# Moving small edge-row copies from GpSimd to ScalarE in a fused Mamba-2 and pooling decoder step

## The chip, the cores and the metric

The kernel runs on one core of a Trainium2 chip. The core's engines work side by side and meet through semaphores: TensorE multiplies matrices (PE for its multiplications, PEld for the loads of its stationary operand), VectorE (DVE), ScalarE (ACT) and GpSimd (POOL) work elementwise on tiles of up to 128 partitions, and SyncE (SP) issues the transfers between memory and the tiles. Each engine works through its own list of instructions in order.

The metric is the device time of one execution in microseconds. The kernel before took 1685.69 us, the median of three runs (1685.56 to 1687.11). The profile shows one more execution, of 1685.18 us.

## What is computed

One step of a decoder of two layers, on 1024 new prompt tokens and on 8 x 8 sample tokens that continue eight older sequences: 1088 token columns. Layer 0 is a Mamba-2 (SSD) mixer, layer 1 a causal pooling mixer; each is normalised, modulated, gated and added to its input. Beside the outputs y, the step returns the new states. Three parts matter here: the causal convolution of width 4 with the last three rows of its input as new state, the windowed means with the last 15 rows of their input as new state, and the input projections that produce both inputs.

```python
# SSD branch; conv_prev is zero for the prompt and state_conv for the samples
zxbcdt = h @ w_in
xbc = zxbcdt[..., D_INNER:D_INNER + CONV_DIM]
xp = jnp.concatenate([conv_prev, xbc], axis=1)
conv = conv_b + sum(xp[:, k:k + L] * conv_w[k] for k in range(4))
new_conv = xp[:, -3:]
xbc_act = jax.nn.silu(conv)          # then the SSD scan, gate, norm, w_out
...
# pooling branch; pool_prev is zero for the prompt and state_pool for the samples
uz = h @ w_in
u, z = uz[..., :2048], uz[..., 2048:]
up = jnp.concatenate([pool_prev, u], axis=1)
cs = jnp.cumsum(up, axis=1)          # with a zero row ahead
for g, w in enumerate((2, 4, 8, 16)):
    win_sum = cs[:, 16:16 + L, sl] - cs[:, 16 - w:16 - w + L, sl]
    pooled[g] = win_sum / cnt - u[..., sl]
mixed = (pooled @ w_group) * ch_scale * jax.nn.silu(z)
return mixed @ w_out, up[:, -15:]
```

The sizes: model width 1024, inner width 2048, convolution width (x, B and C together) 4096 = 32 tiles of 128 channels, pooling width 2048 = 16 tiles of 128 channels. Everything is float32.

## The kernel before

**Layout and precision.** Channels lie on the 128 partitions, tokens on the free axis: a tile is 128 channels by 1088 tokens, the 1024 prompt tokens first. Each float32 factor of a multiplication is held as a rounded high half and a low half of the rest, and each product is three multiplications, high x high, high x low and low x high: L168 to L170 in plain products, which go over the tokens in the chunks `CH` of 364, 364 and 360, and L922 to L924 in fast ones. ACT makes the high half by a copy with rounding, another engine subtracts it from the source to get the low half.

**Fast products.** Pairs of output tiles of the input projections are made by a Strassen-like scheme (`fast_pair`) that forms both tiles from seven half-size products. Each product (`product`) is 2 chunks x 4 blocks x 3 = 24 multiplications of 272 tokens. Its weights are sums and differences of blocks of the two tiles' weights, named `sw` and `wr`, which POOL works out in `w_sums` (L887, L888, L892, L894). Each of the seven then goes through `split_half`: the high half `hi` on ACT (L160), the low half `lo` by a subtraction (L162), on POOL for every split whose number modulo 7 is 3 or 5, on DVE for the other five. The tiles `w` for the split halves have two tags with two buffers each, so that three splits are made ahead of the product that uses them; a split can begin once the product that used its buffer is over. The partial results are read from PE's accumulators by ACT (L948) and added by DVE (L933).

**The stages**, by the time in the profiled execution:
- up to about 270 us: normalisation, the first plain products, then eight fast pairs (`front_pairs`): six of the gate z, and two of the convolution's inputs, whose four tiles make group 0.
- about 270 to 870 us: the scan of group g over its chunks of tokens (`scan_group`) is woven with the projection of group g + 1 (`proj_group`). A group is four convolution tiles; each takes three chunks of plain products, which ACT brings from the accumulators into the tile `raw` (L376 and, for the sample tokens of the last chunk, L378), and then the convolution (`conv_tile`). The scan of the next group begins with transpositions on PE (L509) of the convolution's outputs `xbc`. The exponentials of the scan are ACT's (L516, L534).
- about 870 to 1040 us: the output projection of layer 0.
- about 1040 to 1075 us: two plain pairs of layer 1; 1075 to 1360 us: its other fourteen pairs as fast products (`fast_pairs`), each 7 x 24 = 168 multiplications. A pair is one tile `u` of the pooled input and one of the gate, `pz`. The gate takes a tanh on ACT (L803) and a step on DVE (L804). The pairs come in order of their windows: pairs 0 to 3 window 4, then 8, 16 and 2, four pairs each.
- about 1360 us to the end: the product with `w_group`, the output projection and the last normalisation.

**The convolution tile.** `raw` is 128 x 1115: three columns of state (zeros), 1024 prompt columns, then eight sample sequences of three state columns and eight token columns, 11 each. `proj_begin` clears the three columns on POOL (L354) and copies the sample states from `scv` (L355). `scv` holds the states of a group, and is loaded by SP in `proj_open` (L347) into one of two buffers. `conv_tile` makes the first product on ACT (L332, from `raw` into a second tile `acc`, which has the name raw too), the other three on DVE (L334), copies the new state, 3 prompt columns (L335) and 8 x 3 sample columns (L336), from `raw` into `ncv`, then lets ACT overwrite `raw` by the tanh (L337), and DVE forms the output (L338, L340). The copies must therefore be done before L337. SP stores `ncv` after a group's fourth tile (L363).

**The pooled tile.** `u` is 128 x 1223: 15 columns of zeros, 1024 prompt columns, then 8 sequences of 15 state and 8 token columns. `u_begin` takes a buffer from the wide slots (seven, shared with the sums `ws`), has SP load `spl`, clears 15 columns on POOL (L761) and copies the 8 x 15 states (L762). The fast pair writes the tokens. `u_pool` copies the new state, 15 prompt columns (L777) and 8 x 15 sample columns (L778), into `npl`, which SP stores (L779), and then works on DVE: one to four doubling additions over the whole tile (L784, into `ws`), a correction of the first columns (L789), and the scaling and subtraction into `pl` (L791, L793). After these the buffers of `u` and `ws` are free for a later tile.

**Order.** The framework's scheduler turns the program into one list for each engine, by its own estimate of when things are ready; the program's order alone does not tell an engine's order. On the queues this matters for what stands behind what: SP's list holds the weight loads, the loads and the stores above; ACT's holds the splits' high halves, the tanh steps and the reads from the accumulators.

Of the kernel before, what the change touches and what calls it, by code (L numbers as in the profile page):

```python
# [83 lines left out]
class Build:  # L84
# [241 lines left out]
    def conv_tile(self, ti, raw, dst, ncv):  # L326

        nc, n = self.nc, 1112
        rv = raw[:, 1027:1115].rearrange("p (b w) -> p b w", w=11)
        w = [self.cwh[:, 4 * ti + k:4 * ti + k + 1] for k in range(4)]  # L330
        acc = self.raw_tile()
        nc.scalar.activation(acc[:, :n], raw[:, :n], AF.Identity, bias=self.cwh[:, 128 + ti:129 + ti], scale=w[0])  # L332
        for k in range(1, 4):
            nc.vector.scalar_tensor_tensor(out=acc[:, :n], in0=raw[:, k:k + n], scalar=w[k], in1=acc[:, :n], op0=ALU.mult, op1=ALU.add)  # L334
        nc.gpsimd.tensor_copy(ncv[:, 0:1, :], raw[:, 1024:1027].unsqueeze(1))  # L335
        nc.gpsimd.tensor_copy(ncv[:, 1:9, :], rv[:, :, 8:11])  # L336
        nc.scalar.activation(raw[:, :n], acc[:, :n], AF.Tanh)  # L337
        nc.vector.scalar_tensor_tensor(out=dst[:, :NP], in0=raw[:, :NP], scalar=1.0, in1=acc[:, :NP], op0=ALU.add, op1=ALU.mult)  # L338
        th, v = (t[:, 1027:1115].rearrange("p (b w) -> p b w", w=11)[:, :, 0:8] for t in (raw, acc))
        nc.vector.scalar_tensor_tensor(out=dst[:, NP:TOK].rearrange("p (b i) -> p b i", i=8), in0=th, scalar=1.0, in1=v, op0=ALU.add, op1=ALU.mult)  # L340
# [10 lines left out]
    def proj_begin(self, G, ii):  # L351
        nc = self.nc
        raw = self.raw_tile()
        nc.gpsimd.memset(raw[:, 0:3], 0.0)  # L354
        nc.gpsimd.tensor_copy(raw[:, 1027:1115].rearrange("p (b w) -> p b w", w=11)[:, :, 0:3], G["scv"][:, ii])  # L355
        return raw

    def proj_end(self, G, ii, raw):
# [396 lines left out]
    def u_begin(self, p):  # L755
        nc = self.nc
        raw = self.slots.get("u", wide=True)
        spl = self.gp2.tile([P, 8, 15], F32, tag="spl", bufs=2, name=self.name("spl"))
        nc.sync.dma_start(spl, self.io["spool"][p])
        rv = raw[:, 1039:1223].rearrange("p (b w) -> p b w", w=23)  # L760
        nc.gpsimd.memset(raw[:, 0:15], 0.0)  # L761
        nc.gpsimd.tensor_copy(rv[:, :, 0:15], spl)  # L762
        return raw, rv

    def u_chunk(self, U, ps, ch):
# [6 lines left out]
    def u_pool(self, p, U):  # L772

        nc, gi, (raw, rv) = self.nc, p // 4, U
        w = WINDOWS[gi]
        npl = self.gp2.tile([P, 9, 15], F32, tag="npl", bufs=2, name=self.name("npl"))
        nc.gpsimd.tensor_copy(npl[:, 0:1, :], raw[:, 1024:1039].unsqueeze(1))  # L777
        nc.gpsimd.tensor_copy(npl[:, 1:9, :], rv[:, :, 8:23])  # L778
        nc.sync.dma_start(self.io["npT"][p], npl)  # L779
        s, step, m = raw, 1, WIDE  # L780
        while step < w:
            d = self.slots.get("ws", wide=True)
            m -= step
            nc.vector.tensor_tensor(out=d[:, :m], in0=s[:, :m], in1=s[:, step:step + m], op=ALU.add)  # L784
            if step > 1:
                self.slots.free(s)
            s, step = d, 2 * step
        o = 16 - w
        nc.vector.tensor_tensor(out=s[:, o:o + w - 1], in0=s[:, o:o + w - 1], in1=self.kc[:, K_CNT + 15 * gi:K_CNT + 15 * gi + w - 1], op=ALU.mult)  # L789
        pl = self.slots.get("pl")  # L790
        nc.vector.scalar_tensor_tensor(out=pl[:, :NP], in0=s[:, o:o + NP], scalar=1.0 / w, in1=raw[:, 15:1039], op0=ALU.mult, op1=ALU.subtract)  # L791
        sv = s[:, 1039:1223].rearrange("p (b w) -> p b w", w=23)[:, :, o:o + 8]
        nc.vector.scalar_tensor_tensor(out=pl[:, NP:TOK].rearrange("p (b i) -> p b i", i=8), in0=sv, scalar=1.0 / w, in1=rv[:, :, 15:23],  # L793
                                       op0=ALU.mult, op1=ALU.subtract)
        self.slots.free(raw, s)
        nc.sync.dma_start(self.pld[p], pl)
        self.slots.free(pl)
# [764 lines left out]
```

## Time and profile before

| What | us |
|---|---|
| median of three runs (lowest, highest) | 1685.69 (1685.56, 1687.11) |
| the profiled execution | 1685.18 |
| its span in the profile | 1683.4 |
| busy PE / PEld | 1649.9 / 1556.7 |
| busy DVE / ACT / POOL | 1274.0 / 785.5 / 446.0 |

By stage, in the same execution (busy us):

| stretch, us | PE | DVE | ACT | POOL |
|---|---|---|---|---|
| 0 to 270 | 260.74 | 213.89 | 128.05 | 77.01 |
| 270 to 870 | 594.08 | 471.67 | 400.60 | 140.96 |
| 870 to 1040 | 169.37 | 111.57 | 56.17 | 18.04 |
| 1040 to 1075 | 32.09 | 32.29 | 23.08 | 12.73 |
| 1075 to 1360 | 282.57 | 262.54 | 92.02 | 173.37 |
| 1360 to 1683 | 311.02 | 182.07 | 85.54 | 23.86 |

Busy time counts an engine's instructions, not those that issue transfers or wait. The span runs from the first to the last recorded instruction; the execution's time has 1.78 us more around it. The granted clock of PE was 0.992 of full speed on the mean. A group of instructions is shown as line, engine, operation, output and input by the program's names, partitions x elements of each and the count, then the total and the mean of one in ns, then idle time of the engine just before and what ended it. In the view by time, the first number is the start and the second the duration, both in us; a bracket holds the idle time before it and what ended that. In the view of waits a row gives the waiting engine, tile and line, what it waited for, then the total in us, how often, and the longest.

### The profile page before, as it was taken

To read this page: it belongs to the slowest core of one execution; us is meant where nothing else is said; L and a number is where in the kernel's file an instruction comes from. 1 tells how busy PE (TensorE), PEld (TensorE's weight loads), DVE (VectorE), ACT (ScalarE), POOL (GpSimd) and SP (SyncE) were. 2 spreads that over 40 slices of the span, in tenths; PEclk is the share of its full clock that TensorE was granted. 3 is DMA by queue.
4 is the path that set the end of the run, shared out by engine and by line. 5 is a ranking of instruction groups with operands and counts; after the bars stand their busy time and mean duration, and the time that the engine had idled before them with its cause. 6 is when DMAs were issued, how large, how long until landed. Compare 5 with 4: busy or idle time off the path is not lost.

```text
span 1683.4 us, 30188 instructions
## 1 busy us (share of the span) xinstructions
PE 1649.9 (98%) x11771; PEld 1556.7 (92%) x11771; DVE 1274.0 (76%) x2182; ACT 785.5 (47%) x1539; POOL 446.0 (26%) x467
## 2 busy tenths in 40 slices
PE   8999999999999999999999999999999999999997
PEld 6899999889898888888889998999999999999997
DVE  6897688777778778788787647999999876555545
ACT  6544336767657676767442227533332343122123
POOL 0134440313122231222010022376666620000012
PEclk9999999999999999999999999999999999999998
DMA  8422225445354544445875132132333467411102
GB/s 336 164 89 104 78 80 207 146 145 182 108 171 121 167 127 141 141 123 182 285 247 192 43 116 79 67 125 97 111 110 110 138 250 305 155 52 51 38 26 106
DMA packets 111246, 232.03 MB, mean 138 GB/s; under 512 B 16864, under 2 KB 56960, under 8 KB 111104
## 3 DMA queue, kind: packets, MB, share of 16 engines
q1 hardware_dynamic: 111104, 230.10, 40.2%
q8 instruction: 93, 1.52, 0.4%
q14 instruction: 49, 0.40, 0.1%
HBM read 172.09 MB, written 57.98 MB: 137 GB/s over the span
## 4 chain that ended last, share of the span: by engine, by line
PE 34%; POOL 8%; issue 8%; DVE 5%; DMA 1%; ACT 1%; POOLq 0%; SPq 0%; ACTq 0%; DVEq 0%
PE mm L168 9%; PE mm L169 9%; PE mm L170 9%; POOL w L162 2%; PE st L924 1%; PE st L923 1%; PE st L922 1%; POOL sw L888 1%; POOL sw L887 1%; POOL npl L777 1%; POOL wr L892 1%; POOL npl L778 1%; DVE gl L684 1%; POOL sw L894 1%; PE y L550 0%
## 5 line engine op out<-in xcount | busy, mean ns | idle before, releaser
L168 PE MATMUL mm<-gh,wh 128*128 128x364 f32 (+3 forms) x768 | 254.8, 333 | 1.7 <-DVE x L703 1.3
L169 PE MATMUL mm<-gl,wh 128*128 128x364 f32 (+3 forms) x768 | 254.0, 331 | 2.2 <-DVE gl L684 2.2
L170 PE MATMUL mm<-gh,wl 128*128 128x364 f32 (+3 forms) x768 | 253.7, 331 | 0.0
L168 PE MATMUL mm<-hh,wh 128*128 128x364 f32 x720 | 248.4, 345 | 0.0
L169 PE MATMUL mm<-hl,wh 128*128 128x364 f32 x720 | 239.0, 332 | 0.0
L170 PE MATMUL mm<-hh,wl 128*128 128x364 f32 x720 | 237.6, 330 | 0.0
L703 DVE SCALAR_TENSOR_TENSOR x<-mm,gat,x 128x364 f32<-128x364 f32 (+3 forms) x192 | 108.9, 571 | 148.3 <-PE mm L170 147.9
L924 PE MATMUL st<-hh,w 128*128 128x272 f32 x704 | 203.2, 289 | 0.8 <-DVE w L162 0.8
L923 PE MATMUL st<-hl,w 128*128 128x272 f32 x704 | 203.1, 288 | 0.0
L922 PE MATMUL st<-hh,w 128*128 128x272 f32 x704 | 202.9, 288 | 0.0
L125 ACT ACTIVATE wh<-wr 128x1024 fp32r<-128x1024 f32 x73 | 77.2, 1057 | 224.6 <-PE mm L169 209.1
L924 PE MATMUL st<-t,w 128*128 128x272 f32 x528 | 152.4, 289 | 3.8 <-POOL w L162 2.9
L923 PE MATMUL st<-t,w 128*128 128x272 f32 x528 | 152.2, 288 | 0.7 <-DVE t L1190 0.7
L922 PE MATMUL st<-t,w 128*128 128x272 f32 x528 | 151.7, 287 | 0.0
L168 PEld LDWEIGHTS mm<-gh,wh 128*128 128x128 f32 x768 | 144.8, 189 | 5.4 <-DVE x L703 2.0
L169 PEld LDWEIGHTS mm<-gl,wh 128*128 128x128 f32 x768 | 145.4, 189 | 3.8 <-DVE gl L684 2.8
L170 PEld LDWEIGHTS mm<-gh,wl 128*128 128x128 f32 x768 | 145.5, 189 | 0.3 <-issue 0.2
L563 POOL TENSOR_TENSOR hd<-h,cd 128x256 f32<-128x256 f32 x56 | 67.1, 1198 | 282.4 <-DVE h L564 139.4
L334 DVE SCALAR_TENSOR_TENSOR raw<-raw,cwh,raw 128x1112 f32<-128x1112 f32 x96 | 134.3, 1399 | 9.8 <-ACT raw L332 9.1
L168 PEld LDWEIGHTS mm<-hh,wh 128*128 128x128 f32 x720 | 135.4, 188 | 5.5 <-ACT raw L376 1.6
L169 PEld LDWEIGHTS mm<-hl,wh 128*128 128x128 f32 x720 | 135.5, 188 | 4.6 <-issue 3.0
L170 PEld LDWEIGHTS mm<-hh,wl 128*128 128x128 f32 x720 | 135.3, 188 | 3.0 <-issue 2.9
(267 smaller groups left out, 4060.7 us busy)
## 6 DMA issues: line engine op xcount, KB each, us to landing
wr<-win SPq DMA_DIRECT2D x48, 512.0 KB, 4.8
acb<-acd SPq DMA_DIRECT2D x64, 256.0 KB, 3.9
wr<-pin SPq DMA_DIRECT2D x32, 512.0 KB, 3.6
x<-xT SPq DMA_DIRECT2D x16, 544.0 KB, 7.3
zsd<-z SPq DMA_DIRECT2D x16, 544.0 KB, 2.7
z<-zsd SPq DMA_DIRECT2D x16, 544.0 KB, 5.8
gyd<-xbc SPq DMA_DIRECT2D x16, 544.0 KB, 4.9
gr<-gyd SPq DMA_DIRECT2D x16, 544.0 KB, 4.9
```

The costliest lines, as they stand in the source:

```text
L125: self.nc.scalar.activation(hi[:, :nk, :], raw[:, :nk, :], AF.Copy)
L162: eng.tensor_tensor(out=lo, in0=src, in1=hi.bitcast(F32), op=ALU.subtract)
L168: nc.tensor.matmul(ps[:, :n], hi[:, k, :], ah[:, a:a + n], start=first, stop=False)
L169: nc.tensor.matmul(ps[:, :n], hi[:, k, :], al[:, a:a + n], start=False, stop=False)
L170: nc.tensor.matmul(ps[:, :n], lo[:, k, :], ah[:, a:a + n], start=False, stop=last)
L334: nc.vector.scalar_tensor_tensor(out=acc[:, :n], in0=raw[:, k:k + n], scalar=w[k], in1=acc[:, :n], op0=ALU.mult, op1=ALU.add)
L563: nc.gpsimd.tensor_tensor(out=hd, in0=h, in1=cd.unsqueeze(2).to_broadcast([P, 4, 64]), op=ALU.mult)
L684: nc.vector.scalar_tensor_tensor(out=lo, in0=raw, scalar=scl[:, k:k + 1], in1=hi.bitcast(F32), op0=ALU.mult, op1=ALU.subtract)
L703: ins = nc.vector.scalar_tensor_tensor(out=x[d][:, a:a + pn], in0=ps[:, :pn], scalar=self.gat[l][:, d, 8:9], in1=x[d][:, a:a + pn], op0=AL ...
L922: nc.tensor.matmul(ps[c][:, :QUART], hi[:, k], xh[:, t], start=(k == 0), stop=False)
L923: nc.tensor.matmul(ps[c][:, :QUART], hi[:, k], xl[:, t], start=False, stop=False)
L924: nc.tensor.matmul(ps[c][:, :QUART], lo[:, k], xh[:, t], start=False, stop=(k == 3))
```

## The change

Six copies in three functions go from GpSimd (`nc.gpsimd.tensor_copy`) to ScalarE (`nc.scalar.copy`). Operands, program order, buffers and transfers are the same; the two memsets (L354, L761) stay on GpSimd. The copies run 32 times each in `conv_tile` (two) and `proj_begin` (one), and 16 times each in `u_begin` (one) and `u_pool` (two): 144 in all.

```diff
@@ conv_tile @@
             nc.vector.scalar_tensor_tensor(out=acc[:, :n], in0=raw[:, k:k + n], scalar=w[k], in1=acc[:, :n], op0=ALU.mult, op1=ALU.add)
-        nc.gpsimd.tensor_copy(ncv[:, 0:1, :], raw[:, 1024:1027].unsqueeze(1))
-        nc.gpsimd.tensor_copy(ncv[:, 1:9, :], rv[:, :, 8:11])
+        nc.scalar.copy(ncv[:, 0:1, :], raw[:, 1024:1027].unsqueeze(1))
+        nc.scalar.copy(ncv[:, 1:9, :], rv[:, :, 8:11])
         nc.scalar.activation(raw[:, :n], acc[:, :n], AF.Tanh)
@@ proj_begin @@
         nc.gpsimd.memset(raw[:, 0:3], 0.0)
-        nc.gpsimd.tensor_copy(raw[:, 1027:1115].rearrange("p (b w) -> p b w", w=11)[:, :, 0:3], G["scv"][:, ii])
+        nc.scalar.copy(raw[:, 1027:1115].rearrange("p (b w) -> p b w", w=11)[:, :, 0:3], G["scv"][:, ii])
         return raw
@@ u_begin @@
         nc.gpsimd.memset(raw[:, 0:15], 0.0)
-        nc.gpsimd.tensor_copy(rv[:, :, 0:15], spl)
+        nc.scalar.copy(rv[:, :, 0:15], spl)
         return raw, rv
@@ u_pool @@
-        nc.gpsimd.tensor_copy(npl[:, 0:1, :], raw[:, 1024:1039].unsqueeze(1))
-        nc.gpsimd.tensor_copy(npl[:, 1:9, :], rv[:, :, 8:23])
+        nc.scalar.copy(npl[:, 0:1, :], raw[:, 1024:1039].unsqueeze(1))
+        nc.scalar.copy(npl[:, 1:9, :], rv[:, :, 8:23])
         nc.sync.dma_start(self.io["npT"][p], npl)
```

In the built lists POOL has 144 instructions fewer and ACT as many more; PE's order is the same. On ACT, L335 stands between L378 and L332 of its tile, and L336 and L355 behind L332; L762 of a later pair stands ahead of two weight splits (L160); L777 and L778 come after the last read of the pair's product by ACT. On DVE, in each woven group, a decay step of the scan (L535) comes after L338 and L340. On SP, the load of `scv` (L347) and the store of `ncv` (L363) each stand one place further back, behind a weight load.

## Prediction

> **What bounds the kernel now.** I began with busy time per engine, then took busy time by stretch, because the edited lines lie in two stages with different neighbours: the interleaved stage (state scan with input projection, about 270 to 870 us) and the pool stage's fast products (about 1075 to 1360 us).
>
> ```profile
> span 1683.4 us, 30188 instructions
> PE 1649.9 (98%) x11771; PEld 1556.7 (92%) x11771; DVE 1274.0 (76%) x2182; ACT 785.5 (47%) x1539; POOL 446.0 (26%) x467
> 300.00:700.00 400.00, 399.22 (x3011) 354.84 (x3000) 310.84 (x525) 274.17 (x618) 102.18 (x146) 1.00 0.46 142
> 1126.00:1229.00 103.00, 103.00 (x825) 103.00 (x825) 97.21 (x150) 32.84 (x65) 65.19 (x48) 1.00 0.32 112
> 1229.00:1311.00 82.00, 79.64 (x632) 79.00 (x631) 78.43 (x112) 23.18 (x47) 58.93 (x44) 1.00 0.30 100
> ```
>
> The columns of a stretch are its length, then busy PE, PEld, DVE, ACT and POOL, the granted clock, the DMA share and GB/s. PE is busy for 399.22 of 400 us in the interleaved stage and for all of 1126:1229. Only in 1229:1311 does it miss 82 - 79.64 = 2.36 us, and there DVE is at 78.43 / 82 = 96%. So a change away from PE can win only where PE waits for the engine concerned. The view of waits says how much that is (total, times, longest; the first two rows are the whole run, the rest 1060:1360):
>
> ```profile
> PEld st L924 <- POOL w L162: 3.8, 4, 1.6
> PEld tr L509 <- DVE xbc L338: 1.4, 3, 0.6
> PEld st L924 <- POOL w L162: 2.2, 3, 1.1
> PEld pl L168 <- DVE pz L804: 1.2, 1, 1.2
> PEld st L924 <- POOL u L761: 1.0, 1, 1.0
> PE st L924 <- POOL w L162: 1.5, 2, 0.9
> PE st L924 <- POOL u L761: 0.8, 1, 0.8
> ```
>
> One of these waits, in order of time, on POOL and PE:
>
> ```profile
> 1297.10 1.39 POOL L777 COPY npl<-u 128x15 f32<-128x15 f32 x1
> 1298.45 1.29 POOL L162 TENSOR_TENSOR w<-wr,w 128x512 fp32r<-128x512 f32 x1
> 1299.68 1.49 POOL L778 COPY npl<-u 128x120 f32<-128x120 f32 x1
> 1301.16 1.47 POOL L762 COPY u<-spl 128x120 f32<-128x120 f32 x1
> 1308.02 2.25 POOL L162 TENSOR_TENSOR w<-wr,w 128x512 fp32r<-128x512 f32 x1
> ...
> 1310.32 0.39 PE L924 MATMUL st<-t,w 128*128 128x272 f32 x1 [0.84 <-POOL u L761]
> ```
>
> POOL runs from 1297.10 without a pause to 1310.27, the end of the last L162, and PE, which had waited 0.84 us, starts 0.05 us later. The profile names L761 because it stands next on POOL; what PE needs is the low half of the split weights that L162 writes.
>
> **What the change takes from POOL.** 144 copies:
>
> ```profile
> L778 POOL COPY npl<-u 128x120 f32<-128x120 f32 x16 | 19.5, 1216 | 0.0
> L777 POOL COPY npl<-u 128x15 f32<-128x15 f32 x16 | 17.9, 1124 | 14.9 <-DVE u L933 14.9
> L336 POOL COPY ncv<-raw 128x24 f32<-128x24 f32 x32 | 17.5, 546 | 0.0
> L335 POOL COPY ncv<-raw 128x3 f32<-128x3 f32 x32 | 13.8, 431 | 128.3 <-ACT raw L376 120.3 <-DVE raw L933 8.0
> L355 POOL COPY raw<-scv 128x24 f32<-128x24 f32 x32 | 13.7, 427 | 0.0
> L762 POOL COPY u<-spl 128x120 f32<-128x120 f32 x16 | 11.0, 686 | 0.0
> L777 POOL COPY npl<-u x16: 191/1394/1412, 1063.4 to 1380.3; 128x15 f32<-128x15 f32 x16
> ```
>
> That is 19.5 + 17.9 + 17.5 + 13.8 + 13.7 + 11.0 = 93.4 us of POOL's 446.0. In the sequence above three copies go, 1.39 + 1.49 + 1.47 = 4.35 us, so the last L162 could end at 1305.9. Its high half comes from ACT long before, so the piece is ready 3.5 us ahead of the point where PE wants it (1310.32 - 0.84 = 1309.48). The wait goes whole, and its two fellows in the stretch have the same sequence. By PE's rows the waits on POOL here are 1.5 + 0.8 = 2.3 us, by the weight loads' rows 2.2 + 1.0 = 3.2 us; I take the middle, **-2.7 us**. The remaining 3.8 - 2.2 = 1.6 us is one wait at 240 us, which I leave: POOL there starts its chain late, behind a load.
>
> ```profile
> 235.76 1.29 POOL L887 TENSOR_TENSOR sw<-wr 128x512 f32<-128x512 f32 x1 [4.58 <-DMA wr<-win]
> ```
>
> What is late next is DVE, at 96% of that stretch. It too should gain, since the last row of the copies shows one and the same 15-element copy at 191 and at 1394 ns: it mostly waits for something that DVE holds, and the reverse shows in DVE's rows.
>
> ```profile
> L784 DVE TENSOR_TENSOR ws<-ws 128x1220 f32<-128x1220 f32 x7 | 17.9, 2554 | 0.2
> L784 DVE TENSOR_TENSOR ws<-ws 128x1216 f32<-128x1216 f32 x7 | 10.0, 1425 | 0.2
> ```
>
> The same addition takes 1425 or 2554 ns. I count nothing for it in the forecast, since PE names DVE only once here (L804, 1.2 us); the bounds are 0 and -1.2 us. The Trainium skill, page SBUF — State Buffer, section "SBUF: two separate sides", has the reason: DVE operations with two SBUF inputs and GpSimd instructions share one pair of ports, held exclusively for a whole instruction. By that rule each of the 93.4 us could also have been held against DVE, and it makes the first rival below likelier; 191 against 1394 ns agrees.
>
> **What it gives to ACT.** The trace has no copy of this kind on ACT. The nearest rows bound it:
>
> ```profile
> L534 ACT ACTIVATE cd<-acb 128x4 f32<-128x4 f32 x56 | 11.4, 203 | 17.4 <-POOL hd L563 11.8 <-DMA acb<-acd 5.3
> L322 ACT ACTIVATE hh<-x 128x64 fp32r<-128x64 f32 x16 | 3.7, 246 | 2.7 <-POOL x L321 2.6 <-DVE x L321 0.2
> L516 ACT ACTIVATE M<-acb,tka 128x128 f32<-128x128 f32 x256 | 87.0, 393 | 23.4 <-PE y L550 23.2
> ```
>
> Below stands 203 ns, above 393: between 29 and 57 us for 144 copies. I take 0.20 us for 3 to 24 elements, the row nearest in size (L534), and, an estimate between L322 and L516, 0.29 for 120: 112 x 0.20 + 32 x 0.29 = 31.7 us, which makes ACT 817 us, 49%. In the interleaved stage twelve copies come with each group, 2.4 us in about 75, so ACT goes from 274 to about 287 us of each 400. That lies beside PE's 399 and costs nothing, except in one chain, at a group's border, where the scan needs the convolution that has just begun:
>
> ```profile
> 716.92 0.12 ACT raw L378
> 717.04 0.08 issue
> 717.12 1.33 ACT raw L332
> ```
>
> The convolution's first step L332 is what DVE's three steps, the product L338 and so PE's L509 in the second row of waits hang on. In the changed order the copy L335 stands between L378 and L332. Of its 0.20 us, 0.08 falls into the gap that is there, so about 0.1 us remains at each of the three borders where the waits show L509 behind L338: **+0.3 us**; bounds 0, and 7 borders between the 8 groups at 0.3 (0.39 - 0.08) = 2.1. L336 and L355 follow L332 and lie under DVE's three steps. On DVE, L535 of the scan falls behind L338 and L340 in the groups: L509, which these two release, gains by it, and what L535 feeds lies one short DVE step later in a stage where PE names DVE for 1.4 us in all (second row of waits); I count nothing.
>
> In the pool stage ACT is idle two thirds of the time (32.84 of 103), but it runs in order, and L762 is put ahead of two weight splits. It may write only once DVE is done with the buffer's last user:
>
> ```profile
> 1193.11 0.64 ACT L160 ACTIVATE w<-wr 128x512 fp32r<-128x512 f32 x1 [2.08 <-PE st L924]
> 1196.16 0.64 ACT L160 ACTIVATE w<-sw 128x512 fp32r<-128x512 f32 x1 [2.42 <-PE st L924]
> 1196.94 2.31 DVE L791 SCALAR_TENSOR_TENSOR pl<-ws,u 128x1024 f32<-128x1024 f32 x1
> 1200.57 0.67 DVE L162 TENSOR_TENSOR w<-sw,w 128x512 fp32r<-128x512 f32 x1
> ```
>
> With L762 behind the first of these splits, ACT stands from 1193.75 to 1199.25, 5.5 us, and the next split slips from 1196.16 to about 1199.6, the tanh steps (L803) behind it likewise. I cost it at nothing, because DVE's half of that split stands behind L791 in any case (1200.57), and PE uses the piece three products after its buffer came free, 1196.16 + 3 x 24 matmuls x 0.125 (103 us / 825) = 1205.2, 4.0 us after DVE's half is done at 1201.24. Without that lead it would be up to 5.5 us in each pair.
>
> L777 and L778 wait for the last piece of u and then only delay L948, which PE paces. The stores L363 and L779 follow their copies: SP issued L779 at once behind L778, so it comes earlier, and the weight loads behind it on SP no later. Two other moves on SP cost nothing: the load of scv (L347) and the store of ncT (L363) each fall behind one weight load, while the scv of a group has two buffers and is loaded ahead of its group, and nothing inside the kernel waits for the store.
>
> **Sum.** -2.7 + 0.3 = -2.4 us. The profiled execution took 1685.18 us, 1.78 more than its span, so it would take 1682.8; the three runs' median is 0.51 above it: **1683.3 us**. Own range with the bounds above: -3.2 - 1.2 = -4.4 to -2.3 + 2.1 = -0.2, so 1681.3 to 1685.5.
>
> **Rivals.**
>
> *More comes free.* If POOL's wait at 240 us is also the copies' doing (a chain of them stands 30 us earlier), and DVE, no longer held, gives back L804's wait, it is -(3.2 + 1.6 + 1.2) = -6.0 from 1685.7: **1679.7 us**. For it speak the stretched DVE rows; against it, that POOL idles 4.58 us before L887 there, and that PE's rows leave little else to win.
>
> *ACT's queue becomes the bound.* Mechanism: L762 holds ACT until DVE frees the buffer, and the splits behind it reach PE late. In the pairs with window 16 (1229:1311) the lead is shorter:
>
> ```profile
> 1303.34 0.64 ACT L160 ACTIVATE w<-sw 128x512 fp32r<-128x512 f32 x1 [2.42 <-PE st L924]
> 1310.11 0.71 DVE L162 TENSOR_TENSOR w<-sw,w 128x512 fp32r<-128x512 f32 x1
> ```
>
> This piece has its DVE half at 1310.82 and is due at 1303.34 + 9.0 = 1312.3, 1.5 us later. From a further delay of 1.5 us PE stands still. If the eight pairs of windows 8 and 16 each lose 1 us beyond their lead, it is 8 x 1.0 + 0.3 - 2.7 = +5.6: 1685.7 + 5.6 = **1691.3 us**. For it speaks the hold of 5.5 us in one row; against it, that DVE's own order makes its half late already. The Trainium skill, page PSUM — Partial Sum Buffer, section "Engine vs sequencer instructions", calls ScalarE's queue strictly first in, first out, which is the premise of this rival; no run here shows it otherwise.
>
> *Nothing reaches the end.* DVE at 96% takes POOL's place and PE waits for it instead: 1685.7 us, give or take 0.5.
>
> **Chances.** Small gain 0.39, more comes free 0.30, ACT's queue 0.25, nothing 0.06. A measurement of this kernel tells about 0.2% (3.4 us) from no change. Faster than 1682.3: the second case and a sixth of the first, 0.30 + 0.06 = 0.36. Slower than 1689.1: nearly all of the third, 0.24. Within: 0.40. The range reaches to the second and the third case and half the spread of the three runs (1.55 / 2 = 0.8) past each: 1678.9 to 1692.1.
>
> **What would show it.** Right: in 1060:1360 no wait of PE or PEld on POOL; POOL at about 353 us; the 128x1220 addition nearer to 1425 ns; idle time of ACT before L762 put down to DVE L791 or L784; a clock as before. The size of the copies on ACT is read from their rows: over 0.4 us each my ACT sum is wrong. Wrong: waits of PE on ACT or DVE L162 in 1126:1311, or more than 3 us in all for L509 behind L338; or the pool stage as long as before with DVE named where POOL stood.

## The result, and the profile after

The changed kernel took 1688.08 us (median of 22 runs, 1685.85 to 1691.27), the kernel before beside it 1685.86 us (22 runs, 1684.13 to 1688.04): a ratio of 1.0015, 95% interval 1.0008 to 1.0021. It is slower by about 2.2 us; the prediction was 1683.3 us, faster by 2.4.

The profiled execution took 1688.01 us. First the heads of its page, then busy time by stretch, with the columns as before, then the view of waits for the whole run (first two rows) and for 1060:1365.

```profile
span 1686.2 us, 30201 instructions
PE 1651.1 (98%) x11771; PEld 1557.9 (92%) x11771; DVE 1281.1 (76%) x2182; ACT 803.6 (48%) x1683; POOL 365.4 (22%) x323
```

```profile
300.00:700.00 400.00, 399.31 (x3013) 354.57 (x3012) 314.82 (x527) 280.06 (x680) 70.20 (x83) 1.00 0.45 142
1126.00:1229.00 103.00, 102.91 (x823) 102.69 (x822) 97.76 (x148) 33.56 (x78) 54.26 (x34) 1.00 0.32 112
1229.00:1311.00 82.00, 79.23 (x628) 78.53 (x627) 77.85 (x108) 25.23 (x60) 45.17 (x27) 1.00 0.29 100
```

```profile
PEld st L924 <- POOL w L162: 5.4, 4, 2.1
PEld tr L509 <- DVE xbc L338: 1.4, 3, 0.5
PEld st L924 <- POOL w L162: 3.4, 3, 1.7
PE st L924 <- POOL w L162: 2.8, 2, 1.4
PE st L924 <- POOL u L761: 1.4, 1, 1.4
```

The woven stage is as before: 399.31 us of PE in 400, against 399.22, at the same clock. The loss is in the pool stage. PE's list is the same in both kernels, so the starts of one and the same multiplication can be compared: between the two that run at 1229 and at 1345 us in the kernel before, the changed kernel falls behind by 2.6 us, and at the first of them it is only 0.5 us behind. PE's waits there name POOL as before, and they have grown from 1.5 + 0.8 to 2.8 + 1.4 = 4.2 us, although POOL has 80.6 us less to do (446.0 to 365.4).

Which engine sets the pace there is seen in the length of a pair. One fast pair begins on DVE with one addition of 128x1222 elements, so the first and the last of five such additions span the four window-16 pairs. The rows of that group between 1225 and 1330 us, before and after (count, shortest, median and longest duration in ns, first and last start):

```profile
L784 DVE TENSOR_TENSOR ws<-u x5: 1653/1657/1661, 1230.3 to 1318.9; 128x1222 f32<-128x1222 f32 x5
```

```profile
L784 DVE TENSOR_TENSOR ws<-u x5: 1639/1647/1651, 1232.2 to 1323.9; 128x1222 f32<-128x1222 f32 x5
```

A pair took (1318.9 - 1230.3) / 4 = 22.15 us before and (1323.9 - 1232.2) / 4 = 22.93 us after, where PE needs 168 x 0.125 = 21.0. Busy time from the first of these starts to the last, before and after, and DVE's only wait in that stretch, which reads the same in both:

```profile
1230.35:1318.90 88.55, 86.19 (x685) 85.55 (x684) 83.92 (x124) 26.05 (x53) 59.16 (x45) 1.00 0.32 106
```

```profile
1232.16:1323.86 91.70, 87.50 (x690) 86.46 (x690) 87.05 (x125) 27.97 (x68) 47.36 (x31) 1.00 0.30 102
```

```profile
DVE pz L804 <- ACT zt L803: 4.2, 8, 0.6
```

DVE idles 88.55 - 83.92 = 4.63 us before and 91.70 - 87.05 = 4.65 us after, nearly all of it while ACT makes the tanh of a tile that DVE has just written. So in both kernels these pairs take as long as DVE's own work and that short round to ACT, and they have become longer by what DVE is busy for longer, 3.13 us. PE meanwhile waits 88.55 - 86.19 = 2.36 us and 91.70 - 87.50 = 4.20 us. DVE enters the four pairs 1.9 us later and leaves them 5.0 us later than before. The light pairs of window 2 behind them take part of that back: the span is longer by 2.8 us.

Where DVE loses the 0.8 us of each pair is in one group. The splits of `sw` on DVE in 1229:1345, before and after (total us, mean ns):

```profile
L162 DVE TENSOR_TENSOR w<-sw,w 128x512 fp32r<-128x512 f32 x17 | 13.5, 797 | 0.3 <-ACT w L160 0.3
```

```profile
L162 DVE TENSOR_TENSOR w<-sw,w 128x512 fp32r<-128x512 f32 x17 | 18.1, 1067 | 0.0
```

The same 17 subtractions cost 4.6 us more. The order of time on POOL and DVE in one pair shows which work stretches them. Before:

```profile
1276.33 4.01 DVE L784 TENSOR_TENSOR ws<-ws 128x1220 f32<-128x1220 f32 x2
1278.97 0.11 POOL L761 MEMSET u<- 128x15 f32 x1
1279.02 1.47 POOL L762 COPY u<-spl 128x120 f32<-128x120 f32 x1
1280.26 0.77 DVE L162 TENSOR_TENSOR w<-sw,w 128x512 fp32r<-128x512 f32 x1
1280.45 1.73 POOL L887 TENSOR_TENSOR sw<-wr 128x512 f32<-128x512 f32 x1
1285.89 2.25 POOL L162 TENSOR_TENSOR w<-wr,w 128x512 fp32r<-128x512 f32 x1
```

After, the same pair:

```profile
1279.71 3.86 DVE L784 TENSOR_TENSOR ws<-ws 128x1220 f32<-128x1220 f32 x2
1282.15 0.30 ACT L762 COPY u<-spl 128x120 f32<-128x120 f32 x1 [2.71 <-DVE ws L784]
1282.17 0.11 POOL L761 MEMSET u<- 128x15 f32 x1 [1.34 <-DVE ws L784]
1282.25 2.47 POOL L887 TENSOR_TENSOR sw<-wr 128x512 f32<-128x512 f32 x1
1283.49 1.78 DVE L162 TENSOR_TENSOR w<-sw,w 128x512 fp32r<-128x512 f32 x1
1285.20 2.50 DVE L784 TENSOR_TENSOR ws<-ws 128x1208 f32<-128x1208 f32 x1
1288.80 1.32 POOL L162 TENSOR_TENSOR w<-wr,w 128x512 fp32r<-128x512 f32 x1
```

The row of two L784 holds the second and the third of the pair's four additions; the row of 128x1208 is the fourth. In these rows both engines work by turns. Before, POOL's turn at the end of the third addition went to the copy L762: it stands there for 1.47 us but works for little of it, DVE's L162 follows in 0.77 us, and the weight sum L887 has the turn after. With the copy gone L887 has its turn: it ends at 1284.72, and L162, which began at 1283.49, ends 0.55 us behind that, after 1.78 us. Then L888 stretches the fourth addition just as L887 did before (2.50 against 2.51 us). So DVE meets one long POOL instruction more in each pair. That DVE waits in turn for whole POOL instructions agrees with what the Trainium skill says on the page SBUF — State Buffer, section "SBUF: two separate sides", of the port pair that the two share.

### The profile page after: what moved, and what is told of

Its sections match the earlier page's. It is cut to its first block, busy times and chain, and to the rows that moved or that the text cites. A ratio compares the mean times of both kernels' runs of the same rounds, so it can differ in the third digit from the quotient of the medians.

```text
span 1686.2 us, 30201 instructions
## 1 busy us (share of the span) xinstructions
PE 1651.1 (98%) x11771; PEld 1557.9 (92%) x11771; DVE 1281.1 (76%) x2182; ACT 803.6 (48%) x1683; POOL 365.4 (22%) x323
## 4 chain that ended last, share of the span: by engine, by line
PE 70%; DVE 17%; issue 6%; ACT 3%; POOL 2%; DMA 1%; SPq 0%; POOLq 0%; DVEq 0%; ACTq 0%
PE mm L168 15%; PE mm L169 15%; PE mm L170 15%; PE st L924 4%; PE st L922 3%; PE st L923 3%; DVE ws L784 3%; DVE w L162 3%; PE y L550 2%; PE S L557 2%; DVE u L933 2%; PE y L554 1%; PE am L243 1%; DVE pz L804 1%; DVE pz L933 1%
## 5 line engine op out<-in xcount | busy, mean ns | idle before, releaser
L563 POOL TENSOR_TENSOR hd<-h,cd 128x256 f32<-128x256 f32 x56 | 59.4, 1061 | 378.1 <-DVE h L560 132.2
```

The source lines that it names most:

```text
L563: nc.gpsimd.tensor_tensor(out=hd, in0=h, in1=cd.unsqueeze(2).to_broadcast([P, 4, 64]), op=ALU.mult)
```

## The experiments

Two theories could explain a loss in the pool stage, and a third puts it elsewhere. **Collision on DVE**: the copies on POOL kept the weight sums away from DVE's splits, and DVE sets the pace of the window-16 pairs. **Rival A, ACT's queue**: L762 stands on ACT for 2.71 us until DVE has freed the buffer, and the splits L160 behind it come late. **Rival B**: the convolution's copies ahead of L332 cost at the group borders. The ratios below are to runs of the kernel before on the same chip.

**One stage's copies alone.** The pool stage's three on ACT, the convolution's on POOL:

```diff
-        nc.gpsimd.tensor_copy(rv[:, :, 0:15], spl)
+        nc.scalar.copy(rv[:, :, 0:15], spl)
...
-        nc.gpsimd.tensor_copy(npl[:, 0:1, :], raw[:, 1024:1039].unsqueeze(1))
-        nc.gpsimd.tensor_copy(npl[:, 1:9, :], rv[:, :, 8:23])
+        nc.scalar.copy(npl[:, 0:1, :], raw[:, 1024:1039].unsqueeze(1))
+        nc.scalar.copy(npl[:, 1:9, :], rv[:, :, 8:23])
```

> Only L762, L777 and L778 on ACT; the three convolution copies stay on POOL. Theory (collision on DVE): without the three copies ahead of it POOL's weight sum L887 starts about 4.0 us after the pair's first read of u instead of 6.7 and falls onto DVE's additions and splits, DVE's L162 beside it takes about 1.8 us instead of 0.8, and the window-16 pairs, which DVE paces, take 22.9 us each instead of 22.1: time as the changed kernel, before + 2 to 3 us. Rival A (ACT's queue: L762 waits on ACT for DVE's L784, 2.7 us, and delays the weight splits L160): the same time, before + 2 to 3. Rival B (the convolution's copies ahead of L332 at the group borders cost it): before + 0, window-16 period 22.1.

Measured: 1688.79 us, ratio 1.0015 (1.0006 to 1.0024), the whole loss. The five additions between 1225 and 1330 us:

```profile
L784 DVE TENSOR_TENSOR ws<-u x5: 1641/1644/1649, 1234.7 to 1326.3; 128x1222 f32<-128x1222 f32 x5
```

(1326.3 - 1234.7) / 4 = 22.90 us a pair. L887 starts 4.2 us behind the pair's first read of u here and 5.8 us behind it in the kernel before, where the expectation had 4.0 and 6.7. In this kernel the lists of PE and DVE are those of the kernel before, so a changed order on DVE is not the cause.

And the convolution's three on ACT, the pool stage's on POOL:

```diff
-        nc.gpsimd.tensor_copy(ncv[:, 0:1, :], raw[:, 1024:1027].unsqueeze(1))
-        nc.gpsimd.tensor_copy(ncv[:, 1:9, :], rv[:, :, 8:11])
+        nc.scalar.copy(ncv[:, 0:1, :], raw[:, 1024:1027].unsqueeze(1))
+        nc.scalar.copy(ncv[:, 1:9, :], rv[:, :, 8:11])
...
-        nc.gpsimd.tensor_copy(raw[:, 1027:1115].rearrange("p (b w) -> p b w", w=11)[:, :, 0:3], G["scv"][:, ii])
+        nc.scalar.copy(raw[:, 1027:1115].rearrange("p (b w) -> p b w", w=11)[:, :, 0:3], G["scv"][:, ii])
```

> Only L335, L336 and L355 on ACT; the pool stage's copies stay on POOL. Theory: window-16 period 22.1 us as before, a few tenths won or lost at the group borders, time within 1 us of before. Rival A: the same. Rival B: before + 2 us, with PE's waits near the starts of the groups (281 and 801 us) longer by 2 us in all.

Measured: 1685.83 us, ratio 0.9995 (0.9986 to 1.0004): no difference that these runs can tell. Rival B is out.

**L762 back on POOL**, the other five copies on ACT:

```diff
-        nc.scalar.copy(rv[:, :, 0:15], spl)
+        nc.gpsimd.tensor_copy(rv[:, :, 0:15], spl)
```

> As the changed kernel, but L762 back on POOL, where it stands between the memset L761 and L887. Theory: the copy takes the turn beside DVE's second L784, about 1.4 us, L887 starts that much later, DVE's L162 goes ahead of it at about 0.8 us, and the window-16 period is 22.0 to 22.2 us: before - 0.5 to + 0.5. Rival A: ACT is free of the hold, so the same, 22.1. Rival B: as the changed kernel less what lies in the pool stage, before + 2.

Measured: 1685.84 us, ratio 0.9994 (0.9985 to 1.0003). The five additions:

```profile
L784 DVE TENSOR_TENSOR ws<-u x5: 1649/1653/1660, 1233.5 to 1321.4; 128x1222 f32<-128x1222 f32 x5
```

(1321.4 - 1233.5) / 4 = 21.98 us a pair. The loss hangs on this one copy, but the collision and rival A both said so.

**An idle copy on POOL** tells them apart. To the changed kernel comes a copy of 15 cleared columns into a tile that nothing reads; the lists of PE, DVE, ACT and SP are those of the changed kernel, with L762 on ACT.

```diff
-        nc.scalar.copy(rv[:, :, 0:15], spl)
+        nc.scalar.copy(rv[:, :, 0:15], spl); gap = self.gp2.tile([P, 15], F32, tag="gap", bufs=1, name=self.name("gap")); nc.gpsimd.tensor_copy(gap, raw[:, 0:15])
```

> The changed kernel with one more POOL copy, 128x15 from the columns that L761 has cleared into a tile that nothing reads, right behind L761; the lists of the other engines are the same, so L762 still holds ACT. Theory (collision on DVE): the idle copy takes the turn that L887 had, L887 starts 1.2 to 1.5 us later, DVE's L162 is back at about 0.8 us, the window-16 period at 21.9 to 22.2, and the time is 2 to 3 us under the changed kernel although POOL has more to do. Rival A (ACT's queue): nothing on ACT is changed, so the period stays 22.9 or grows and the time stays at that of the changed kernel or above. Rival B: the time stays.

Measured: 1684.45 us, ratio 0.999 (0.9981 to 0.9998): the loss is gone. By the ratios that is 2.5 per thousand under the changed kernel, about 4 us, more than the 2 to 3 expected. The waits of ACT ahead of L762 for L784 in 1229:1345 are nearly what they were, first in the changed kernel, then here (total, times, longest):

```profile
ACT u L762 <- DVE ws L784: 15.5, 5, 4.8
```

```profile
ACT u L762 <- DVE ws L784: 13.6, 5, 3.7
```

Here are the turns of one pair, the splits of `sw` on DVE in 1229:1345, the five additions, and busy time over the four pairs:

```profile
1275.74 3.86 DVE L784 TENSOR_TENSOR ws<-ws 128x1220 f32<-128x1220 f32 x2
1278.38 1.28 POOL L762 COPY gap<-u 128x15 f32<-128x15 f32 x1
1279.52 0.68 DVE L162 TENSOR_TENSOR w<-sw,w 128x512 fp32r<-128x512 f32 x1
1279.62 1.74 POOL L887 TENSOR_TENSOR sw<-wr 128x512 f32<-128x512 f32 x1
1280.13 2.50 DVE L784 TENSOR_TENSOR ws<-ws 128x1208 f32<-128x1208 f32 x1
```

```profile
L162 DVE TENSOR_TENSOR w<-sw,w 128x512 fp32r<-128x512 f32 x17 | 13.5, 792 | 0.3 <-ACT w L160 0.3
```

```profile
L784 DVE TENSOR_TENSOR ws<-u x5: 1648/1651/1655, 1230.2 to 1317.9; 128x1222 f32<-128x1222 f32 x5
```

```profile
1230.24:1317.86 87.62, 85.77 (x681) 85.12 (x680) 82.98 (x125) 28.26 (x68) 52.38 (x37) 1.00 0.33 107
```

The idle copy takes the turn of the old one, L162 is back at 0.68 us in this pair and at 792 ns on the mean, and a pair takes (1317.9 - 1230.2) / 4 = 21.93 us. The 1.00 us that a pair gains (22.93 - 21.93) is the 1.10 us that L162 gains here (1.78 - 0.68), to a tenth. DVE again idles 87.62 - 82.98 = 4.64 us in the four pairs. ACT still stands ahead of L762, and it costs nothing: rival A is out. Work was added on POOL, and the kernel became faster than the changed one.

That it comes out under the kernel before as well is not shown to be the idle copy's doing. The profiled execution is 1.4 us shorter than that of the kernel before (spans 1682.0 and 1683.4), but by the starts of the same multiplications all of this lies ahead of 1126 us, and from there to the end the two are level within 0.1 us. Two profiled executions of one and the same kernel (the kernel before in mixed order, below) part by 1.3 us ahead of 1126 us.

**Two idle copies**, the second one behind the first in the program:

```diff
-        ...; nc.gpsimd.tensor_copy(gap, raw[:, 0:15])
+        ...; nc.gpsimd.tensor_copy(gap, raw[:, 0:15]); nc.gpsimd.tensor_copy(gap, raw[:, 0:15])
```

> As the kernel with one idle POOL copy behind L761, with a second one behind the first. Theory: the second takes one more of POOL's turns beside DVE's L162, L887 starts 0.7 to 1.3 us later still and DVE's third L784 comes back from 2.5 us towards 1.3; the window-16 period is 21.0 to 21.9 us and the time 0 to 2 us under the kernel with one, unless POOL's L162, later by as much, is then what PE waits for: period 22.0 to 23.0 and 0 to 3 us over it. Rival A: no difference between one and two.

Measured: 1685.21 us, ratio 1.0005 (0.9995 to 1.0015). The scheduler put the second copy behind L887, so L887 did not move: the experiment did not try what it was made for. DVE's L162 stays at 0.68 us, and the window-16 pairs took 22.08 us ((1318.7 - 1230.4) / 4 by the same rows). That lies in the range of the second branch, 22.0 to 23.0, by luck: what is longer is DVE's correction L789, 1.06 us instead of 0.91, and 0.15 us is what a pair takes more than with one copy. Over four pairs that is 0.6 us; the rest of the 1.5 per thousand between the two ratios, whose intervals overlap, is not explained.

**Less work for DVE.** The kernel with one idle copy, and one split of seven more on POOL:

```diff
-POOLW = (3, 5)
+POOLW = (2, 3, 5)
```

> The kernel with one idle POOL copy, and the split with number 2 modulo 7 subtracted on POOL as well (POOLW = (2, 3, 5)), in the stretch in which POOL idles 7.5 us ahead of L894. Theory (DVE's work sets the window-16 period): DVE is free of 0.68 us in each pair, the period goes from 21.9 to 21.2 to 21.4 us and the time 1 to 3 us under the kernel with one idle copy. Rival C (POOL's chain sets the pace): POOL's chain is 1.3 us longer, the period 22 to 23, and the time 1 to 4 us over it.

Measured: 1690.46 us, ratio 1.0026 (1.0014 to 1.0038). The total went the way of rival C and beyond its 1 to 4 us: 3.6 per thousand over the kernel with one idle copy. But here too the scheduler moved the idle copy behind L887, so the collision at L162 was back. The window-16 pairs:

```profile
1285.16 2.49 POOL L887 TENSOR_TENSOR sw<-wr 128x512 f32<-128x512 f32 x1
1286.42 1.78 DVE L162 TENSOR_TENSOR w<-sw,w 128x512 fp32r<-128x512 f32 x1
1287.60 0.66 POOL L762 COPY gap<-u 128x15 f32<-128x15 f32 x1
1288.12 1.41 DVE L784 TENSOR_TENSOR ws<-ws 128x1208 f32<-128x1208 f32 x1
```

```profile
L784 DVE TENSOR_TENSOR ws<-u x5: 1589/1592/1644, 1236.4 to 1325.5; 128x1222 f32<-128x1222 f32 x5
```

```profile
1236.45:1325.53 89.08, 84.64 (x671) 83.79 (x670) 81.93 (x121) 28.14 (x68) 57.73 (x41) 1.00 0.33 105
```

A pair takes (1325.5 - 1236.4) / 4 = 22.28 us, 0.65 under the changed kernel's 22.93. That this is near the 0.68 us of the split is chance. The idle copy has taken the turn of L888, so the fourth addition takes 1.41 us instead of 2.50, and a gate step L804 takes 0.81 instead of 0.44. DVE is busy for 81.93 / 4 = 20.48 us of a pair instead of 21.76, 1.28 less, but it idles 1.79 us instead of 1.16, because it now waits for the tanh three times in a pair (6.5 us in twelve waits). So work taken from DVE shortens a pair only by what does not come back as a longer wait for ACT. Other pairs lost time: between the multiplications that run at 1126 and at 1229 us in the kernel before, this one falls behind by 2.6 us, the changed kernel by 0.4. PE's waits for POOL's L162 in 1060:1370 are larger than in the changed kernel (4.8 us under that name against 2.8). These were not taken apart.

**Other neighbours for the window-16 pairs.** If DVE sets the pace only where heavy pairs follow each other, the order of the pairs should take it away:

```diff
+ORD = (2, 3, 4, 8, 12, 5, 9, 13, 6, 10, 14, 7, 11, 15)
...
-        for p in range(2, 16):
+        for p in ORD:
             items += [(io["pin"][8 * (p // 4) + p % 4 + i], 0) for i in (0, 4)]
...
-        for p in range(PLAIN, 16):
+        for p in ORD:
```

In the changed kernel:

> The changed kernel with its fourteen fast pairs in another order, 2, 3, 4, 8, 12, 5, 9, 13, 6, 10, 14, 7, 11, 15, so that no two pairs of window 16 follow each other; everything else is as in the changed kernel. Theory (DVE sets the pace only while several window-16 pairs of 22.9 us follow each other): every pair takes 20.9 to 21.3 us, PE's own pace, and the 5.6 us that pairs 6 to 11 took over six times 21.03 shrink to under 1.5: 4 to 5.5 us under the changed kernel. Rival A (ACT's hold by L762 costs, whatever stands next): the loss stays, within 1 us of the changed kernel. Rival C (POOL's own chain sets the pace): the loss stays, pairs of 22.9 us come singly.

In the kernel before:

> The kernel before with the same order of pairs. Theory: its pairs 8 to 10 took 22.1 us where PE needs 21.03; mixed, they all take about 21.0 to 21.3, before - 2 to - 3 us, and so within 1 us of the changed kernel in the same order: the place of the copies is then worth nothing either way. Rival A: within 1 us of before, and 2 us or more under the changed kernel in the same order. Rival C: within 1 us of before.

Measured: 1684.83 us with the copies on ACT, ratio 0.9995 (0.9986 to 1.0004), and 1681.53 us with the copies on POOL, 0.998 (0.9971 to 0.999). Busy time in 1126:1360, for the changed kernel in its own order, the changed kernel mixed, and the kernel before mixed:

```profile
1126.00:1360.00 234.00, 229.71 (x1823) 228.28 (x1822) 216.72 (x332) 77.13 (x178) 121.56 (x77) 1.00 0.33 113
```

```profile
1126.00:1360.00 234.00, 233.61 (x1867) 233.39 (x1866) 215.76 (x335) 80.85 (x183) 123.28 (x78) 1.00 0.34 115
```

```profile
1126.00:1360.00 234.00, 234.00 (x1872) 234.00 (x1871) 209.30 (x332) 74.37 (x146) 147.92 (x114) 1.00 0.33 116
```

PE misses 4.3 us of this stretch in the changed kernel, 0.4 when mixed, and none in the kernel before mixed; DVE, at 93% and 92% in the first two, is at 89% in the last. The theory's first half holds: a light pair absorbs what a heavy one leaves. With the copies on ACT a window-16 pair still takes DVE 22.95 us, but the pair of window 2 behind it takes 18.41 and the one behind that 21.60, together PE's pace of three times 21.0. The gain on the changed kernel is 2.0 per thousand by the ratios, 3.4 us, where 4 to 5.5 was expected. The theory's second half, that the place of the copies is then worth nothing, missed: the medians lie 3.3 us apart where 1 was allowed. By the starts of the same multiplications the two profiled executions, 2.4 us apart, part by 0.7 us between 1126 and 1229 us, not at all between 1229 and 1345, and by 0.95 us right behind the last pair, where PE waits 0.7 us for ACT's L1020 with the copies on ACT and not for it with them on POOL. What holds L1020 up was not looked into. The other 0.7 us lie ahead of 1126 us, within what two executions of one kernel differ by there.

**Mixed order with some of the copies.** All three ran on one chip, with the edits above combined: the convolution's copies on ACT; all but L762 on ACT; and the kernel before mixed once more.

> The mixed order of pairs with the three convolution copies on ACT and the three of the pool stage on POOL. Theory: every pair at 21.03 us as in the kernel before in mixed order, no wait of PE on POOL in the pool stage, and the convolution's copies worth nothing: before - 3 to - 4 us, within 1 us of the repeat below. Rival (the copies on ACT cost in the woven stage what the kernel before in mixed order did not show): 1 to 2 us above the repeat.

> The mixed order with all copies on ACT but L762, which stays on POOL between L761 and L887. Theory: L887 starts behind that copy, a window-16 pair takes 22.0 us instead of 22.9 and its lighter neighbour the rest, so before - 2.5 to - 4 us, 0.5 to 1.5 us under the changed kernel in mixed order. Rival (the mixed order takes all of the collision, wherever it stands): as the changed kernel in mixed order, before - 0.3 to - 2.

> The kernel before in mixed order once more, for a second sample beside the two others: before - 3 to - 4 us by its first runs. If it comes out within 1.5 us of before, the first was chance.

Measured: 1682.55 us, ratio 0.9977 (0.9968 to 0.9986); 1684.34 us, 0.999 (0.9981 to 0.9999); and 1684.03 us, 0.9985 (0.9976 to 0.9994). The first lies 1.5 us under the third, where within 1 us was expected, but their intervals overlap, so the convolution's copies again show no certain worth. L762 on POOL, expected 0.5 to 1.5 us under the changed kernel in mixed order, is 0.5 per thousand under it by the two ratios, which overlap as well; its 1.8 us under the kernel before are less than the 2.5 to 4 expected and lie in the range of the rival. The repeat came to 2.2 us under the kernel before instead of 3 to 4, which is still more than the 1.5 that would have called the first sample chance. The mixed order is a gain of 1.5 to 2.3 per thousand in all three samples that have the pool stage's copies on POOL. The lowest ratio is the first (mixed order, the convolution's copies on ACT, the pool stage's on POOL), but it is not shown to be better than the kernel before in mixed order.

## Why the prediction was wrong

The measured 1688.08 us lies above the prediction's own range of 1681.3 to 1685.5. The wide range, 1678.9 to 1692.1, holds it only because it was drawn around the rivals; none of its cases gave such a time for the reason that the runs show.

**What bounds the kernel: wrong at one place.** PE waits for POOL's L162, that is so, but in the window-16 pairs POOL was not what set the pace. The prediction's own row of 1229:1311 had DVE at 96%, and it called DVE "late next". DVE was already the pace: it idles the same 1.16 us of a pair before, after and with the idle copy, so that a pair grows from 22.15 to 22.93 us with one collision more and shrinks to 21.93 without it, and PE's wait on POOL is all but gone when light pairs stand between.

**"The wait goes whole", -2.7 us: the step that failed.** The wait did not go, it grew by 1.9 us (PE's 2.3 to 4.2). The sum moved POOL's chain forward by the 4.35 us of three copies and took every other duration from the rows of before. In the pair shown, L887 starts 1282.25 - 1279.71 = 2.54 us behind the start of DVE's row of two additions instead of 1280.45 - 1276.33 = 4.12, and L162 ends 10.41 us behind it instead of 11.81: the chain came forward by 1.4 us, not by 4.35. The copies had mostly been waiting; with them gone, the memset L761 ahead of L887 waits for DVE's second addition, 1.34 us in this pair and 5.4 us in four waits. And what did come forward were the weight sums L887, L888 and L892, which stand between the last two POOL rows of the prediction's sequence and are not shown in it: L887 fell on DVE's L162 and made DVE's pair 0.78 us longer. POOL alone could not have taken the whole wait away: with the idle copy, without the collision, a pair still takes 21.93 us where PE needs 21.0, and PE still waits 87.62 - 85.77 = 1.85 us in the four pairs.

**"What is late next is DVE. It too should gain": the wrong sign.** I had read the stretched rows (a copy at 191 or 1394 ns, an addition at 1425 or 2554) as copies holding up DVE, bounds 0 and -1.2 us. The turns show the reverse: a small copy waits long and holds DVE for little, a weight sum of 512 columns holds it for over a microsecond. The 128x1220 addition did not come near 1425 ns. In the changed kernel, by group in the prediction's window 1166:1310:

```profile
L784 DVE TENSOR_TENSOR ws<-ws 128x1220 f32<-128x1220 f32 x7 | 16.8, 2398 | 0.2
```

It went from 2554 to 2398 ns only: in both kernels POOL's subtraction L162 stands beside it (in the pair shown, from 1276.31 before and from 1278.35 after), and the change leaves that on POOL.

The upper bound should have been above nothing: in each of four or five pairs one more POOL instruction against DVE, some 1 us each.

**ACT's copies: right in size.** The forecast was 0.20 us for 3 to 24 elements and 0.29 for 120, 31.7 us in all:

```profile
L355 ACT COPY raw<-scv 128x24 f32<-128x24 f32 x32 | 6.7, 208 | 1.5 <-PE tr L397 1.0 <-DVE xbc L340 0.4
L336 ACT COPY ncv<-raw 128x24 f32<-128x24 f32 x32 | 6.4, 201 | 0.0
L335 ACT COPY ncv<-raw 128x3 f32<-128x3 f32 x32 | 6.2, 194 | 0.3
L762 ACT COPY u<-spl 128x120 f32<-128x120 f32 x16 | 4.8, 297 | 56.5 <-DVE pl L791 29.1 <-DVE ws L784 15.5 <-DVE pz L933 6.9
L778 ACT COPY npl<-u 128x120 f32<-128x120 f32 x16 | 4.7, 299 | 0.0
L777 ACT COPY npl<-u 128x15 f32<-128x15 f32 x16 | 3.1, 203 | 6.4 <-DVE u L933 6.4
```

They sum to 6.7 + 6.4 + 6.2 + 4.8 + 4.7 + 3.1 = 31.9 us. ACT as a whole came to 803.6 us, not 817, since neighbouring rows overlap in time (L762 above, 0.30 us from 1282.15, and the split behind it from 1282.35); and POOL to 365.4 instead of 353, since its 44 subtractions L162 went from 69.1 to 78.8 us. L762's hold is there too, 56.5 us in 15 waits, 3.8 us each where the prediction's one example had 5.5, and costing it at nothing was right: with it a window-16 pair took 21.93 us (one idle copy), without it 21.98 (L762 back on POOL).

**The borders, +0.3 us: not seen.** PE's waits for L509 behind L338 are 1.4 us in three times, as before, and the convolution's copies alone change nothing that can be told.

**The wait at 240 us: rightly left.** It grew from 1.6 to 2.1 us, and POOL's start there hangs on the load as before:

```profile
235.77 1.29 POOL L887 TENSOR_TENSOR sw<-wr 128x512 f32<-128x512 f32 x1 [5.06 <-DMA wr<-win]
```

PE came 0.6 us earlier (at 239.44 instead of 240.05) to a point that a transfer fixes, and so the rival that counted it among the gains fell.

**The rivals.** The one that forecast a loss named the wrong engine: it priced 1 us in each of eight pairs by ACT's queue. That its size per pair was near is luck, its mechanism was not there. "DVE takes POOL's place" named the right engine, and gave it no price of its own because it took DVE's work as fixed. The prediction's signs of being wrong would not have led to DVE either: they looked for waits of PE on ACT or on DVE's L162, and in 1126:1311 there is one, of 0.3 us of a weight load, while PE's own waits went on naming POOL.

## What to carry to other kernels

An engine whose list gets shorter does not only finish earlier, its long instructions also move, and what they then stand beside can be worth more than what was taken away: look for each large instruction at its new neighbours on any engine that it takes turns with. Where an engine is at 96% in a stretch, count its work per round before pricing a wait on another engine, since the wait may only show who is released last in a round that the full engine sets. And where heavy rounds follow each other, an order that mixes them with light ones may be worth more than the finer edits.

## What the runs showed of the hardware

A POOL copy of 15 columns that did nothing useful took the changed kernel from 1.0015 (1.0008 to 1.0021) to 0.999 (0.9981 to 0.9998) of the time before. Its row had 0.20 us in the median and 1.28 us where it stood beside DVE's addition, yet DVE's split behind it took 0.68 us; in its absence a 128x512 weight sum took the turn and the split 1.78. DVE and POOL with operands in SBUF took turns instruction by instruction in these rows, so the cost of a POOL instruction to DVE was what it had to do in its turn, not the time that the profile gives it.
